# Two-layer decoder trunk: the second pair's values by quarters, two products sent to DRAM, four split tiles

## The chip, the cores and the metric

The kernel runs on one core of a Trainium2 chip. The metric is the device time of one execution in microseconds; of three runs of the kernel before, the median is 1551.42 us (1542.9 to 1553.19). Five engines work beside each other: TensorE (PE, matmuls), VectorE (DVE), ScalarE (ACT), GpSimd (POOL, here little more than an issuer of accumulating DMAs) and SyncE (SP, issuer of loads).

## The reference

Two layers over 512 tokens of width 1024. Each layer has a mixer (sliding-window attention and a retention, gated and merged) and an MLP; the change lies in the MLP and in the end of the program.

```python
def hybrid_layer(x, g_mix, w_in, sinks, w_a, w_b, w_out, g_mlp, w_up, w_down):
    h = rmsnorm(x, g_mix)
    z = h @ w_in
    ...
    mixed = jax.nn.sigmoid(ga) * ya + jax.nn.sigmoid(gb) * yb
    x = x + mixed @ w_out

    h2 = rmsnorm(x, g_mlp)
    x = x + jnp.square(jax.nn.relu(h2 @ w_up)) @ w_down
    return x

def reference(x, ...):
    for l in range(DEPTH):
        x = hybrid_layer(x, ...)
    return rmsnorm(x, g_final)
```

`w_up` is 1024 x 4096 and `w_down` 4096 x 1024. Everything is float32.

## The kernel before

**Split operands.** A float32 product is made of three matmuls: each operand is split into a high part (`hi`, `xh`, `r`) that the fast matmul format holds, and a low rest (`lo`, `xl`, `r`); `products` (L315) issues high x high, high x low and low x high, which are lines L321, L322 and L323. Weights come as units of 128 x 1024. For each, SP loads a tile `raw`; ACT writes `hi` (L275), DVE writes `lo` (L276). `unit` (L282) hands out one unit and splits up to two units beyond it; `split_until` (L259) loads up to four units beyond the one that it splits. There are six `raw` tiles and three of `hi` and of `lo`.

**The MLP.** x is held transposed in SBUF (8 tiles of 128 x 512). The 4096 hidden columns are eight blocks of 512 (`e` = 0 to 7). Because relu squared is homogeneous, the RMS factor is not put on the input: it is applied to the finished sum as a per-token `factor`, the inverse of mean square plus epsilon.

Products of 2 x 2 halves are computed by a scheme of seven products with sums of operands (Strassen-Winograd) in place of eight. For `e` > 0 two calls of `pair` (L1049) make the hidden values, 256 hidden columns each, from weight units with three and a half times 24 matmuls of 256 columns, in banks `a`, `e` and `b`, with `eu` as a holding place for two of them and `z` (128 x 2 x 512) for the result. `sums` holds the split sums of x's halves. `keep_up` (L1025) squares z. For the first pair it splits the left half of z (`first_hi`, `first_lo`) and the first sum; for the second pair it makes the other three sums (`Forms.rest`, L427), splits them, and splits z itself into `u_two`. For block 0, `group` makes four 128-column chunks in four PSUM banks together and `put_up` calls `keep_up` after chunks 1 and 3.

`down` (L1084) then multiplies with the block's part of `w_down` in seven steps of 12 matmuls of 512 columns: `b11` (first pair's left half), `u_forms[0]` (P5), `u_forms[1]` (giving U2), `b21`, `u_forms[2]`, `b22`, `u_forms[3]`. PSUM banks `a`, `b`, `c` come in twos, m = 0 and 1. P5 and U2 are copied from PSUM to SBUF by ACT. Four results per m (quadrants (0,0), (1,1), (0,1), (1,0) of tokens by columns) go through a `sink`: `Adding` (blocks 0 to 6) evacuates each to a tile `t`, by ACT where nothing is added, by DVE where P5 or U2 is added, and POOL sends it to a DRAM tile `y` with an adding DMA (L1148; block 0 writes plainly). `Ending` (block 7) loads `y` back, scales it by `factor` (`scale_all`; in the last layer `add_x` does it together with x), adds the last block's products on DVE (L1203, L1204). In layer 0 the result is transposed on PE and added to x (`turn`), and the next layer's first inputs are made (`ready`, `carry`); in the last layer x is transposed on PE and added to y (`add_x`, L1192 and L1196), then squared and summed (L1206), and the final norm and gain are applied (`output`, L1211) and stored.

**Buffers.** `temp` (tag `t`) has seven 128 x 512 tiles, which `eu`, P5, U2, the outgoing `y` tiles and short-lived others share in turn. `big` has six of 128 x 1024.

**Order.** The program is traced in the order of the source, and a scheduler then places the instructions on each engine by its own estimate of times. Each engine works through its list in order. A DMA that adds into DRAM is made to wait, on POOL, for earlier ones to the same rows.

Of the kernel before, what the change touches and what calls it, by code (L numbers as in the profile page):

```python
# [51 lines left out]
AHEAD = 5  # L52
# [51 lines left out]
def decoder(ctx, tc, xT, x_first, w_in, w_a, w_b, w_out, w_up, w_pair, w_down, tables, decay, band, g_last, out):  # L104
# [46 lines left out]
    def raw_tile():  # L151
        return wpool.tile([P, UNIT], F32, tag="raw", name="raw", bufs=6)
# [106 lines left out]
    def split_until(n):  # L259
        while state["split"] < min(n, len(order)):  # L260
# [8 lines left out]
            hi = wpool.tile([P, UNIT], F32R, tag="hi", name="hi")  # L269
            lo = wpool.tile([P, UNIT], F32R, tag="lo", name="lo")  # L270
# [128 lines left out]
    class Forms:  # L399
# [27 lines left out]
        def rest(self, ks, b, d, js):  # L427
            t1, t2, t3, t4 = (self.f[j // 2][:, 2 * (j % 2) : 2 * (j % 2) + 2, :] for j in range(4))
            b12, b21, b22 = b[:, :, H:], d[:, :, :H], d[:, :, H:]
            nc.vector.scalar_tensor_tensor(t2, t1, -1.0, b22, ALU.mult, ALU.subtract)  # L430
            self.keep(ks, 0, self.f[0], js)
            nc.vector.tensor_tensor(t3, b22, b12, ALU.subtract)
            nc.vector.scalar_tensor_tensor(t4, t2, -1.0, b21, ALU.mult, ALU.subtract)
            self.keep(ks, 2, self.f[1], (2, 3))
# [37 lines left out]
    class Rms:  # L472
# [8 lines left out]
        def finish(self):  # L481
            self.value = tmp.tile([P, T], F32, tag="rstd", name="rstd", bufs=2)
# [5 lines left out]
    def layer_body(layer):  # L488
# [501 lines left out]
        last = layer == DEPTH - 1  # L990
        sums = Forms((0, 2))
# [4 lines left out]
        columns = small.tile([P, 2 * NB], F32, tag="columns", name="columns", bufs=1)  # L996
        factor, negative = columns[:, :NB], columns[:, NB:]

        def column_factors():
# [4 lines left out]
            nc.vector.tensor_scalar(factor, ps[:, :NB], 1.0 / D, EPS, ALU.mult, ALU.add)  # L1004
            nc.vector.reciprocal(factor, factor)
            nc.vector.tensor_scalar(negative, factor, -1.0, None, ALU.mult)
            return ps

        def sum_input(ks):
# [7 lines left out]
            sums.rest(ks, *b, (0, 1))  # L1017
# [7 lines left out]
        def keep_up(z):  # L1025
            nc.scalar.activation(z, z, AF.Square)
            if not kept:
                split(first_hi, first_lo, z[:, :, :H])
                u_forms.one(0, z)
                u_forms.keep(0, 0, u_forms.f[0], (0,))  # L1030
                kept.append(z)
            else:
                u_forms.rest(0, kept.pop(), z, (1,))
                split(u_two[:, 0:2, :], u_two[:, 2:4, :], z)
# [3 lines left out]
        def put_up(c):  # L1038
            def put(ps):
# [4 lines left out]
                if c % 2:  # L1044
                    keep_up(z)
# [3 lines left out]
        def pair():  # L1049
# [20 lines left out]
            nc.scalar.activation(z[:, 0, :H], a, AF.Relu)  # L1070
            part = unit("pair", layer)
# [4 lines left out]
            nc.scalar.activation(z[:, :, H:], z[:, :, H:], AF.Relu)  # L1076
            part = unit("pair", layer)
            multiply(b, part, True, sums[3], False)
            nc.scalar.activation(z[:, 1, :H], b, AF.Relu, scale=-1.0)
            keep_up(z)  # L1080

        y = dram.tile([P, NB, D], F32, name=f"y{layer}")

        def down(e):  # L1084
# [22 lines left out]
            for m in range(2):  # L1107
                nc.scalar.activation(p5[m], c[m], AF.Copy)
# [21 lines left out]
        class Adding:  # L1130
# [7 lines left out]

            def put(self, i, j, m, ps, sign, more=None):
                t = temp("y")  # L1140
                if more is None:
                    nc.scalar.activation(t, ps, AF.Copy, scale=float(sign))  # L1142
                elif sign > 0:
                    nc.vector.tensor_tensor(t, ps, more, ALU.add)
                else:
                    nc.vector.scalar_tensor_tensor(t, ps, -1.0, more, ALU.mult, ALU.subtract)
                how = {"accum_op": ALU.add} if self.e else {}
# [4 lines left out]
        class Ending:  # L1152


            def __init__(self, e):
                sums.free()
                self.y, self.done = {}, {}
# [5 lines left out]
                if last:  # L1163
                    self.gain = big("gain")
                    nc.sync.dma_start(self.gain, g_last)
                    self.sq = small.tile([P, 4 * NB], F32, tag="sq", name="sq", bufs=1)
                else:
                    self.scale_all()

            def scale_all(self):  # L1170
# [4 lines left out]

            def begin(self, step):
                if last:
                    if step < 4:
                        self.add_x(*QUADS[step])
                elif step > 1:  # L1180
# [5 lines left out]

            def add_x(self, i, j):
                for m in range(2):
                    ps = bank(ps_mm if m else ps_aux, "xt")
                    block = 2 * j + m  # L1190
                    for k in range(4):
                        nc.tensor.transpose(  # L1192
                            ps[:, k * P : (k + 1) * P], x[:, 4 * i + k, block * P : (block + 1) * P], ident
                        )
                    v = self.y[i, j, m]
                    nc.vector.scalar_tensor_tensor(v, v, factor[:, block : block + 1], ps, ALU.mult, ALU.add)  # L1196

            def put(self, i, j, m, ps, sign, more=None):
# [6 lines left out]
                if last:  # L1205
                    nc.scalar.activation(temp("junk"), v, AF.Square, accum_out=self.sq[:, 2 * block + i : 2 * block + i + 1])  # L1206
                    self.done[i, j] = m
                    if (1 - i, j) in self.done and self.done[1 - i, j] >= m:
                        self.output(j, m)

            def output(self, j, m):  # L1211
                block = 2 * j + m
                total = self.sq[:, 2 * NB + block : 2 * NB + block + 1]
                nc.vector.tensor_tensor(total, self.sq[:, 2 * block : 2 * block + 1], self.sq[:, 2 * block + 1 : 2 * block + 2], ALU.add)
                nc.scalar.activation(total, total, AF.Sqrt, bias=eps, scale=1.0 / D)
                nc.vector.reciprocal(total, total)
                for i in range(2):
                    v = self.y[i, j, m]
                    nc.vector.scalar_tensor_tensor(v, v, total, self.gain[:, i, :], ALU.mult, ALU.mult)
                    (nc.sync if i else nc.scalar).dma_start(out[:, block, i * T : (i + 1) * T], v)  # L1220
# [15 lines left out]
            def ready(self, k):  # L1236
                scaled_input(k, g_mix + 2)
                squared_input(k, g_mix + 2)
                nc.sync.dma_start(spill[:, k, :], x[:, k, :])

            def carry(self):
                self.turn(1, 0)
                for k in range(4, KD):
                    self.ready(k)

        def first_hooks():
# [6 lines left out]
            def at1():  # L1253
                nc.tensor.matmul(used[0], ones, xh[:, 0, :], start=True, stop=True)
# [175 lines left out]
```

## Time and profile before

| | |
|---|---|
| runs, us | 1542.9, 1551.42, 1553.19 |
| profiled execution, us | 1553.22 |
| its span, us | 1551.4 |
| mean granted TensorE clock | 0.988 |
| MLP of layer 0 | about 422 to 757 us of the span |
| MLP of layer 1 | about 1186 us to the end |

The page gives one execution. A row of waits reads: engine, tile and line that waited, engine (or DMA), tile and line that ended the wait, total us, times, longest. A row of the timeline gives start, length, engine, line, operation, output and input tiles, count, and in brackets the idle time before it and what ended it. The row of a DMA queue has packets, MB and the share of 16 engines' time. PE's busy time includes pipelined matmuls' modelled ends, so the steps from start to start tell its pace.

### The profile page before, as it was taken

What the parts mean: (1) busy time and instruction counts of PE and PEld (TensorE: products, weight loads), DVE (VectorE), ACT (ScalarE), POOL (GpSimd) and SP (SyncE); (2) the same over time, 40 slices, a digit from 0 to 9 for tenths busy, and PEclk for the clock granted to TensorE, in tenths of its full rate; (3) what the DMA queues carried; (4) which work ended last, traced back from release to release, by engine and by line L of the source; (5) the groups of instructions that cost most, each with busy time, mean ns of one, the idle gap of its engine ahead of it and who ended that gap; (6) DMA issues with size and microseconds to landing.
All of it is one profiled execution on the core that took longest, in us unless ns stands there. A gap on an engine that the chain in (4) does not pass through costs nothing.

```text
span 1551.4 us, 21097 instructions
## 1 busy us (share of the span) xinstructions
PE 1488.0 (96%) x7766; PEld 1267.4 (82%) x7766; DVE 1108.5 (71%) x1622; ACT 900.0 (58%) x1429; POOL 172.5 (11%) x261
## 2 busy tenths in 40 slices
PE   9999999999999999999899999999999988999995
PEld 7888888888877888888788888888887877888884
DVE  6877567744867777767988765776557777777778
ACT  6657354622666676666765653554345756666664
POOL 0001111100011111111001012110000111001110
PEclk9999999999999999999999999999999999999998
DMA  7654998564235567776647489877532565566772
GB/s 255 196 154 139 264 253 214 154 195 129 96 116 145 160 172 183 184 184 171 236 124 199 126 224 261 206 185 202 157 115 75 175 143 134 156 166 184 183 194 99
DMA packets 92023, 267.88 MB, mean 173 GB/s; under 512 B 10640, under 2 KB 10768, under 8 KB 87824
## 3 DMA queue, kind: packets, MB, share of 16 engines
q1 hardware_dynamic: 63424, 172.94, 33.4%
q0 software_dynamic: 27776, 92.29, 28.2%
q8 instruction: 61, 1.00, 0.2%
q10 hardware_dynamic: 720, 1.31, 0.2%
q14 instruction: 42, 0.34, 0.1%
HBM read 230.32 MB, written 96.47 MB: 211 GB/s over the span
## 4 chain that ended last, share of the span: by engine, by line
PE 66%; issue 18%; DMA 4%; DVE 4%; ACT 4%; POOL 2%; DVEq 0%; ACTq 0%; SPq 0%; POOLq 0%
PE mm L323 18%; PE mm L321 18%; PE mm L322 18%; DMA y<-y 3%; POOL y L1148 2%; PE rv L321 2%; PE rv L322 2%; PE rv L323 2%; ACT hi L275 1%; DVE lo L276 1%; DMA dm<-decay_in 1%; PE score L660 1%; PE b L321 1%; PE pT L625 1%; PE b L322 1%
## 5 line engine op out<-in xcount | busy, mean ns | idle before, releaser
L275 ACT ACTIVATE hi<-raw 128x1024 fp32r<-128x1024 f32 (+1 forms) x366 | 373.2, 1020 | 400.6 <-PE mm L322 251.2
L276 DVE TENSOR_TENSOR lo<-raw,hi 128x1024 fp32r<-128x1024 f32 (+1 forms) x367 | 428.0, 1171 | 200.5 <-ACT hi L275 199.2
L323 PE MATMUL mm<-xh,lo 128*128 128x512 f32 (+1 forms) x1008 | 356.7, 357 | 8.9 <-DVE lo L276 8.9
L321 PE MATMUL mm<-xh,hi 128*128 128x512 f32 (+1 forms) x1008 | 356.8, 357 | 2.3 <-ACT xh L331 2.3
L322 PE MATMUL mm<-xl,hi 128*128 128x512 f32 (+1 forms) x1008 | 358.0, 357 | 0.5 <-DVE xl L332 0.5
L321 PE MATMUL mm<-r,hi 128*128 128x256 f32 (+1 forms) x768 | 252.7, 329 | 3.6 <-ACT mm L1063 3.6
L322 PE MATMUL mm<-r,hi 128*128 128x256 f32 (+1 forms) x768 | 252.0, 328 | 0.0
L323 PE MATMUL mm<-r,lo 128*128 128x256 f32 (+1 forms) x768 | 252.0, 328 | 0.0
L323 PEld LDWEIGHTS mm<-xh,lo 128*128 128x128 f32 x1008 | 191.5, 190 | 38.9 <-DVE lo L276 13.2
L321 PEld LDWEIGHTS mm<-xh,hi 128*128 128x128 f32 x1008 | 191.5, 190 | 28.7 <-ACT xh L331 3.4
L322 PEld LDWEIGHTS mm<-xl,hi 128*128 128x128 f32 x1008 | 191.8, 190 | 25.8 <-DVE xl L332 0.8
L1148 POOL DMA_DIRECT2D y<-y x112 | 93.6, 997 | 660.4 <-ACT y L1142 612.8
L321 PEld LDWEIGHTS mm<-r,hi 128*128 128x128 f32 x768 | 146.9, 191 | 17.8 <-ACT mm L1063 4.7
L322 PEld LDWEIGHTS mm<-r,hi 128*128 128x128 f32 x768 | 146.8, 191 | 12.8
L323 PEld LDWEIGHTS mm<-r,lo 128*128 128x128 f32 x768 | 146.8, 191 | 12.6
L321 PE MATMUL mm<-hi,r 128*128 128x512 f32 x256 | 96.8, 407 | 27.0 <-ACT r L328 27.0
L322 PE MATMUL mm<-lo,r 128*128 128x512 f32 x256 | 102.1, 399 | 0.0
L323 PE MATMUL mm<-hi,r 128*128 128x512 f32 x256 | 101.1, 407 | 0.8 <-DVE r L329 0.5
L321 PE MATMUL b<-hi,r 128*128 128x512 f32 x192 | 79.1, 412 | 4.7 <-ACT r L328 3.5
L321 PEld LDWEIGHTS mm<-hi,r 128*128 128x128 f32 x256 | 47.5, 194 | 41.1 <-ACT r L328 33.6
L322 PE MATMUL b<-lo,r 128*128 128x512 f32 x192 | 77.3, 402 | 0.0
L323 PE MATMUL b<-hi,r 128*128 128x512 f32 x192 | 72.3, 390 | 0.0
(204 smaller groups left out, 2161.9 us busy)
## 6 DMA issues: line engine op xcount, KB each, us to landing
raw<-w_in_in SPq DMA_DIRECT2D x89, 512.0 KB, 5.2
sums_down<-w_down_in POOLq DMA_DIRECT2D x32, 1024.0 KB, 10.8
sums_up<-w_pair_in POOLq DMA_DIRECT2D x56, 512.0 KB, 9.8
y<-y POOLq DMA_DIRECT2D x112, 256.0 KB, 7.3
raw<-w_down_in SPq DMA_DIRECT2D x48, 512.0 KB, 5.1
raw<-w_pair_in SPq DMA_DIRECT2D x84, 256.0 KB, 3.9
raw<-sums_down SPq DMA_DIRECT2D x32, 512.0 KB, 5.2
raw<-sums_up SPq DMA_DIRECT2D x56, 256.0 KB, 4.3
```

Of the source, the lines that this page charges most:

```text
L275: nc.scalar.activation(hi[:, at], raw[:, at], AF.Copy)
L276: nc.vector.tensor_tensor(lo[:, at], raw[:, at], f32(hi[:, at]), ALU.subtract)
L321: nc.tensor.matmul(ps, ah, bh, start=start and i == 0, stop=False, **more)
L322: nc.tensor.matmul(ps, ah, bl, start=False, stop=False, **more)
L323: nc.tensor.matmul(ps, al, bh, start=False, stop=stop and i == n - 1, **more)
L625: nc.tensor.transpose(pt[:, i * P : (i + 1) * P], sm[:, at : at + P], ident)
L660: nc.tensor.matmul(ps[:, g * w : (g + 1) * w], q_s[g][:, c, at], part[:, keys], start=i == 0, stop=i == 1)
L1148: nc.gpsimd.dma_start(y[:, 2 * j + m, i * T : (i + 1) * T], t, **how)
```

## The change

- `second`, `second_late` and `second_rest` replace the second half of `keep_up`: the second pair's value is squared and split in pieces as its quarters are finished, row 0's left half after the second part, the right halves after the third, row 1's left half at the end. `Forms.rest` becomes `middle` and `rest`.
- In `Adding`, P5 (with sign −1) and U2 are sent to DRAM as transfers of their own (`early`), so that all evacuations are plain ACT copies; each block has twelve transfers where it had eight.
- `hi` and `lo` have four tiles each and `raw` five; splitting runs three units ahead (`SPLIT`), loading three beyond that (`AHEAD`). `rstd` has one tile.
- Block 0 makes its chunks two by two (`two_chunks`), with `w_up` laid out to match.
- In the last layer, x is transposed during block 0, divided by `factor` and written to `y` (`turn_x`), and all later transfers add to it; `add_x` is gone. The end applies the gain on DVE before the norm is known and the norm on ACT after.
- `carry` makes all four inputs of the next layer before it squares them.

```diff
-AHEAD = 5
+AHEAD = 4
+SPLIT = 3
...
-        return wpool.tile([P, UNIT], F32, tag="raw", name="raw", bufs=6)
+        return wpool.tile([P, UNIT], F32, tag="raw", name="raw", bufs=5)
...
-            hi = wpool.tile([P, UNIT], F32R, tag="hi", name="hi")
-            lo = wpool.tile([P, UNIT], F32R, tag="lo", name="lo")
+            hi = wpool.tile([P, UNIT], F32R, tag="hi", name="hi", bufs=SPLIT + 1)
+            lo = wpool.tile([P, UNIT], F32R, tag="lo", name="lo", bufs=SPLIT + 1)
...
-        split_until(i + 3)
+        split_until(i + SPLIT + 1)
...
-    def two_chunks(name, layer, moving, evacuates):
+    def two_chunks(name, layer, moving, evacuates, meanwhile=None):
...
+            if meanwhile and u == 0:
+                meanwhile()
...
+        def middle(self, ks, b, d, js):
+            b12, b22 = b[:, :, H:], d[:, :, H:]
+            nc.vector.scalar_tensor_tensor(self.part(1), self.part(0), -1.0, b22, ALU.mult, ALU.subtract)
             self.keep(ks, 0, self.f[0], js)
+            nc.vector.tensor_tensor(self.part(2), b22, b12, ALU.subtract)
+
+        def rest(self, ks, d, js):
+            nc.vector.scalar_tensor_tensor(self.part(3), self.part(1), -1.0, d[:, :, :H], ALU.mult, ALU.subtract)
+            self.keep(ks, 2, self.f[1], js)
...
-            self.value = tmp.tile([P, T], F32, tag="rstd", name="rstd", bufs=2)
+            self.value = tmp.tile([P, T], F32, tag="rstd", name="rstd", bufs=1)
...
+        def turn_x(ps, b, i):
+            for k in range(4):
+                nc.tensor.transpose(ps[:, k * P : (k + 1) * P], x[:, 4 * i + k, b * P : (b + 1) * P], ident)
+            t = temp("y")
+            nc.scalar.activation(t, ps, AF.Copy, scale=inverse[:, b : b + 1])
+            nc.gpsimd.dma_start(y[:, b, i * T : (i + 1) * T], t)
...
-        def keep_up(z):
+        def first_two(z):
             nc.scalar.activation(z, z, AF.Square)
...
+        def second(z, rows, at):
+            nc.scalar.activation(z[:, rows, at], z[:, rows, at], AF.Square)
+            split(u_two[:, rows, at], u_two[:, slice(rows.start + 2, rows.stop + 2), at], z[:, rows, at])
+
+        TWO, LATE, SOON = slice(0, 2), slice(H, T), slice(0, H)
+
+        def second_late(z):
+            second(z, TWO, LATE)
+            u_forms.middle(0, kept[0], z, (1,))
+            u_forms.keep(0, 2, u_forms.f[1], (2,))
+
+        def second_rest(z):
+            kept.pop()
+            u_forms.rest(0, z, (3,))
...
             nc.scalar.activation(z[:, 0, :H], a, AF.Relu)
+            if which:
+                second(z, slice(0, 1), SOON)
...
             nc.scalar.activation(z[:, :, H:], z[:, :, H:], AF.Relu)
+            if which:
+                second_late(z)
...
             nc.scalar.activation(z[:, 1, :H], b, AF.Relu, scale=-1.0)
-            keep_up(z)
+            if which:
+                second(z, slice(1, 2), SOON)
+                second_rest(z)
+            else:
+                first_two(z)
...
             for m in range(2):
-                nc.scalar.activation(p5[m], c[m], AF.Copy)
+                sink.early(1, 1, m, p5[m], c[m], -1)
             multiply(b, u_forms[1], False)
             for m in range(2):
-                nc.scalar.activation(u2[m], b[m], AF.Copy)
+                sink.early(0, 1, m, u2[m], b[m], 1)
...
+            def early(self, i, j, m, t, ps, sign):
+                nc.scalar.activation(t, ps, AF.Copy, scale=float(sign))
+                self.send(i, j, m, t, last or self.e > 0)
+
             def put(self, i, j, m, ps, sign, more=None):
                 t = temp("y")
-                if more is None:
-                    nc.scalar.activation(t, ps, AF.Copy, scale=float(sign))
-                elif sign > 0:
-                    nc.vector.tensor_tensor(t, ps, more, ALU.add)
-                else:
-                    nc.vector.scalar_tensor_tensor(t, ps, -1.0, more, ALU.mult, ALU.subtract)
-                how = {"accum_op": ALU.add} if self.e else {}
+                nc.scalar.activation(t, ps, AF.Copy, scale=float(sign))
+                self.send(i, j, m, t, last or self.e > 0 or more is not None)
+
+            def send(self, i, j, m, t, add):
+                how = {"accum_op": ALU.add} if add else {}
                 nc.gpsimd.dma_start(y[:, 2 * j + m, i * T : (i + 1) * T], t, **how)
...
-                    nc.scalar.activation(temp("junk"), v, AF.Square, accum_out=self.sq[:, 2 * block + i : 2 * block + i + 1])
...
+                    nc.scalar.activation(temp("junk"), v, AF.Square, accum_out=both if ready else first)
+                    nc.vector.tensor_tensor(v, v, self.gain[:, i, :], ALU.mult)
+                    if not ready:
+                        nc.vector.tensor_scalar(first, first, 1.0 / D, EPS, ALU.mult, ALU.add)
+                        return
+                    nc.scalar.activation(total, both, AF.Sqrt, bias=first, scale=1.0 / D)
+                    nc.vector.reciprocal(total, total)
+                    for n in (1 - i, i):
+                        v = self.y[n, j, m]
+                        nc.scalar.activation(v, v, AF.Copy, scale=total)
+                        (nc.sync if n else nc.scalar).dma_start(out[:, block, n * T : (n + 1) * T], v)
...
                 for k in range(4, KD):
-                    self.ready(k)
+                    scaled_input(k, g_mix + 2)
+                for k in range(4, KD):
+                    self.rest(k)
...
-                group("w_up", layer, xs, [put_up(c) for c in range(4)], first_hooks())
+                hooks = first_hooks()
+                for c in (0, 2):
+                    two_chunks("w_up", layer, xs, [put_up(c), put_up(c + 1)], hooks[c // 2])
             else:
-                pair()
-                pair()
+                pair(0)
+                pair(1)
```

More of the change, by code (lines that the diff above doesn't have):

```diff
@@ L1174, in scale_all, with early @@
                         nc.scalar.activation(v, v, AF.Copy, scale=factor[:, 2 * j + m : 2 * j + m + 1])
+            def early(self, i, j, m, t, ps, sign):
+                nc.scalar.activation(t, ps, AF.Copy)
             def begin(self, step):
[L1177 to L1180, printed above, removed]
+                if not last and step > 1:
                     self.turn(*QUADS[step - 2])
@@ L1205, in put @@
                 if last:
[L1206 to L1220 removed]
+                    first, total, both = (self.sq[:, n * NB + block : n * NB + block + 1] for n in range(3))
+                    ready = (1 - i, j, m) in self.done
+                    self.done.add((i, j, m))
+                    nc.scalar.activation(temp("junk"), v, AF.Square, accum_out=both if ready else first)
[9 more added lines that the diff above has]
+                        (nc.sync if n else nc.scalar).dma_start(out[:, block, n * T : (n + 1) * T], v)
             def turn(self, i, j):
@@ L1253, in at1 @@
             def at1():
-                nc.tensor.matmul(used[0], ones, xh[:, 0, :], start=True, stop=True)
+                if last:
+                    used.append(bank(ps_aux, "xt"))
+                    for n in range(KD):
+                        turn_x(used[n % 2], n // 2, n % 2)
+                for ps in used:
+                    nc.tensor.matmul(ps, ones, xh[:, 0, :], start=True, stop=True)
                 sum_input(2)
```

66 lines of the change are left out of this document (26 added, 40 removed).

## The prediction

> **What bounds the kernel now.** I read the page's head first, then what TensorE (PE) waited for, and then the same waits by stage.
>
> ```profile
> span 1551.4 us, 21097 instructions
> PE 1488.0 (96%) x7766; PEld 1267.4 (82%) x7766; DVE 1108.5 (71%) x1622; ACT 900.0 (58%) x1429; POOL 172.5 (11%) x261
> ...
> PE mm L321 <- ACT r L328: 27.0, 16, 1.9
> PE mm L323 <- DVE lo L276: 8.9, 8, 2.3
> PE mm L321 <- ACT mm L1063: 3.6, 4, 1.7
> PE b L321 <- ACT r L328: 3.5, 13, 0.3
> ...
> PE mm L321 <- ACT r L328: 14.2, 8, 1.9
> ...
> PE mm L321 <- ACT r L328: 12.4, 7, 1.9
> ```
>
> PE is busy 96% of the span, so the time is the matmuls plus PE's stops. The first group of waits is the whole kernel; the last two lines are its largest entry again, for 422 to 757 us and 1186 to 1516 us, the two MLP stages. 26.6 of its 27.0 us lie there: the stops are in the eight MLP blocks of each layer (16 waits, 16 blocks), and the mixers have next to none. So the change can win only in the MLPs.
>
> One such stop, first on PE, then on ScalarE (ACT), below two narrow matmuls of a pair; columns are start and length in us, and in brackets the idle time before:
>
> ```profile
> 549.43 0.28 PE L321 MATMUL mm<-r,hi 128*128 128x256 f32 x1
> 549.55 0.28 PE L322 MATMUL mm<-r,hi 128*128 128x256 f32 x1
> ...
> 571.07 0.39 PE L322 MATMUL mm<-lo,r 128*128 128x512 f32 x1
> 571.30 0.39 PE L323 MATMUL mm<-hi,r 128*128 128x512 f32 x1
> 573.44 0.50 PE L321 MATMUL mm<-hi,r 128*128 128x512 f32 x1 [1.76 <-ACT r L328]
> 573.78 0.39 PE L322 MATMUL mm<-lo,r 128*128 128x512 f32 x1
> ...
> 574.24 0.40 PE L322 MATMUL mm<-lo,r 128*128 128x512 f32 x1
> 574.91 0.50 PE L321 MATMUL b<-hi,r 128*128 128x512 f32 x1 [0.27 <-ACT r L328]
> 575.25 0.40 PE L322 MATMUL b<-lo,r 128*128 128x512 f32 x1
> ...
> 570.02 0.36 ACT L1079 ACTIVATE z<-mm 128x256 f32<-128x256 f32 x1
> 570.41 1.06 ACT L1026 ACTIVATE z<-z 128x1024 f32<-128x1024 f32 x1
> 571.38 1.07 ACT L1108 ACTIVATE eu<-mm 128x512 f32<-128x512 f32 x2
> 572.33 1.06 ACT L328 ACTIVATE r<-z 128x1024 fp32r<-128x1024 f32 x1
> ```
>
> After the second pair's last product ACT does a relu, squares the whole 128x1024 value, copies P5 out, and splits the whole value. The split ends at 573.39, and PE, out of other work since 571.30, starts at 573.44. That is the wait of every block.
>
> **What the change takes away.** 512-wide matmuls start 571.30 − 571.07 = 0.23 us apart, 256-wide ones 0.12. The stop costs more than its idle time: 571.30 to 573.44 is 2.14 us for a wait of 1.76, and the next step is 0.34; the second stop takes 0.67 and then 0.34. Over a plain 0.23 that is 0.15 + 0.11 + 0.17 + 0.11 = 0.54 us of refilling a block, some 8 us in 15 blocks.
>
> After such stops PE also runs at half rate for a while, here in the block before, where starts come 0.43 apart:
>
> ```profile
> 531.41 0.80 PE L321 MATMUL b<-hi,r 128*128 128x512 f32 x1 [0.27 <-ACT r L328]
> 532.00 0.63 PE L322 MATMUL b<-lo,r 128*128 128x512 f32 x1
> 532.43 0.63 PE L321 MATMUL b<-hi,r 128*128 128x512 f32 x1
> 532.86 0.63 PE L322 MATMUL b<-lo,r 128*128 128x512 f32 x1
> ...
> 422.00:757.00 335.00, 314.39 (x1893) 275.05 (x1892) 247.75 (x293) 224.58 (x338) 47.72 (x57) 0.98 0.62 168
> 1186.00:1516.00 330.00, 307.64 (x1854) 270.96 (x1853) 234.76 (x278) 213.40 (x321) 46.81 (x56) 0.97 0.60 160
> 539.00:582.50 43.50, 41.47 (x260) 36.71 (x259) 33.13 (x40) 30.47 (x46) 8.21 (x10) 1.00 0.65 174
> ```
>
> In the last three lines (window, length, busy of PE, PEld, DVE, ACT, POOL, granted clock, DMA share, GB/s) the two MLPs have clocks of 0.98 and 0.97. Time lost is 0.02 x 335 + 0.03 x 330 = 16.6 us, by rounding 13 to 20; I take 14, and three quarters of it, 11 us, for the stops of the split (30.5 us of the 43 us of waits listed above). The Trainium skill, "TensorE: Matmul & The Clock Gate", section "Why this matters for your kernels", asks for no idle gaps over about 3 us, so by its rule a 1.76 us wait would cost no clock. Here the clock does fall behind stops of 1.76 and 0.27 us, so the trace does not bear it out; a rival below takes the other side.
>
> In the changed program the first-pair products, b11 and u_forms[0], stand on PE before the second pair's last product. Behind that product nothing is needed at once but row 0 of the second pair's value, which `second` squares and splits a quarter of a block earlier. Only the 128x256 corner of row 1 is left: relu 0.36, square and split of the same width about 0.37 each, by the 128x256 row at 570.02. PE meets it after 6 + 4 + 2 + 8 matmuls, 20 x 0.23 = 4.6 us. Even with ACT's queued work before it (an unpack of weights 1.06, two copies of 0.54) it is there after some 3.5 us. So the wait goes; if ACT ran 1.2 us later than so, it would begin to come back. In the first block of each layer four relus and squares stand together as now, with 24 x 0.23 = 5.5 us of b11 and u_forms[0] as cover; I leave 1 us there. Gain: 27.0 + 3.5 − 2 = 28.5 us.
>
> Next is the start of a pair, 8.9 + 3.6 = 12.5 us in the list. It comes from buffers that a DMA holds:
>
> ```profile
> 580.41 1.08 ACT L1142 ACTIVATE y<-mm 128x512 f32<-128x512 f32 x2
> ...
> 589.66 1.09 ACT L1142 ACTIVATE y<-b 128x512 f32<-128x512 f32 x2 [3.24 <-DMA y<-y]
> ...
> 581.35 2.65 POOL L1148 DMA_DIRECT2D y<-y  x3 [31.91 <-ACT y L1142]
> ...
> ACT y L1142 <- DMA y<-y: 32.8, 11, 3.8
> ...
> y<-y POOLq DMA_DIRECT2D x112, 256.0 KB, 7.3
> ```
>
> ACT stands 3.2 us until the second y(0,0) tile, issued about 581.9, has landed (7.7 us), and the weight splits queue behind it. A fourth split tile puts one more unit of weights, 24 x 0.12 = 2.9 us of pair matmuls, between that stop and PE, and DVE no longer waits for these buffers. Those 12.5 us go.
>
> **What it adds.** ACT takes over four 128x512 evacuations a block from DVE (0.54 us each in the pairs above) and about five small pieces, some 3 us on 30.5 busy in a block of 43.5, DVE loses as much: neither becomes the bound. P5 and U2 go out as accumulating DMAs, twelve a block for eight. All seven temp buffers are now freed by landings; twelve y tiles and two `eu` make exactly two rounds. So the last y(1,0) takes the buffer of the first y(0,0), and the next pair's `eu` that of the second. Between those copies PE has 24 x 0.12 + 12 x 0.23 = 5.6 us; the landing takes 7.7 and the issue about 1, so ACT still stands about 3 us, as now. What hangs on it is the copy that frees bank b: 3 us, then two `eu` copies (0.37, as the relu of 0.36 above) and an unpack (1.06, as the split of that width), 4.8 us, against 36 matmuls of 0.12 = 4.3 us of cover. That is 0.5 us a block; with twelve transfers queued I take 1.0, 14 us in 14 blocks. From below: nothing, if landings take 5 us. From above: 3 us a block, 42 us, if the whole stop showed. The Trainium skill, "DMA: Bandwidth & Descriptors", section "Anatomy of one DMA — SWDGE (gpsimd) path", has a fit of 2 us plus the bytes over 436 GB/s, 2.6 us for 256 KB; by that the ring would cost nothing and my sum be 14 us lower, but the landings here take 7.3.
>
> A put to quadrant (1,1) waits on POOL until P5 has landed in the same rows, with all later y transfers queued behind it; P5 leaves some 11 us earlier, more than 7.7, so nothing. Four more transfers on the DMA rings: the share is 0.65 of 43.5 us, 28 us a block; eight y are some 12 us of it (28.4% in the queue line below), four more 6 us, so 34 of about 40: hidden.
>
> ```profile
> q0 software_dynamic: 1152, 2.10, 28.4%
> ...
> 1535.75 0.60 PE L1192 MATMUL xt<-ident,x 128*128 128x128 f32 x4
> 1536.11 0.48 PE L321 MATMUL b<-hi,r 128*128 128x512 f32 x1
> ...
> 1537.35 0.40 PE L323 MATMUL b<-hi,r 128*128 128x512 f32 x1
> ...
> 1546.45 1.42 DVE L1219 SCALAR_TENSOR_TENSOR y<-y,sq,gain 128x512 f32<-128x512 f32 x2
> ...
> L1220 SPq DMA_DIRECT2D y_out<-y x4: 332/334/350, 1543.5 to 1547.9; - x4
> ```
>
> The transposes of x, eight groups of four at 0.36 (1536.11 − 1535.75), 2.9 us, move from the last block to the last layer's first: no change in sum, and their ACT copies and plain DMAs lie beside PE there. At the end, PE stops at 1537.7, and 13.7 us follow. In the changed program seven gain multiplications (0.71, by the pair of 1.42) and the reciprocals stand on DVE after the last put, then eight ACT multiplications (0.54), then four issues on ACT's queue (0.33): 0.9 + 5.0 + 0.3 + 4.3 + 1.3, and 1551.4 − 1547.9 = 3.5 us from the last issue to the end as now, 15.3: +1.5 us. The order of `carry` at the layer boundary may save 1 us; `w_up` by twos has the same matmuls, and the smaller `raw` and `rstd` rings free as early, since splitting runs a unit ahead.
>
> **Sum.** −28.5 − 8 − 11 − 12.5 + 14 + 1.5 − 1 = −45.5 us. The profiled execution took 1553.2 us, 1.8 above its span, which gives 1508; it lies 1.8 above the median of the runs, 1551.4, and against that it is 1506. Of three runs the fastest took 1542.9, as if with fewer slow stretches of the clock than the profiled one had; for that I give back 3 us and say 1509.
>
> **Rivals.** (1) The clock's half-rate stretches do not hang on these stops, the page's side: then 11 us stay, 1520. For it: the block of 539 to 582.5 us has the same 1.76 us stop and a clock of 1.00. (2) The buffer ring shows in full: +28 us over the forecast, 1537. For it: ACT's 3.2 us stops in 11 of 14 blocks; against: the weights are a unit further ahead. (3) Slower: the accumulate queue. Twelve transfers of some 2 us each in a burst make y(0,0) land late, the first `eu` of the next pair stands, and bank b with it. Each us of landing beyond the 8.2 that my 1.0 us stands for costs 14 us; the 42 us of the forecast are gone at 11.2 us. At the longest landing of a y transfer now,
>
> ```profile
> DMA to landing us min/median/max: 4.6/7.6/12.6
> ```
>
> 12.6 us (505 to 760 us, the last of a burst of eight), it gives 14 x 4.4 = 62 us more, 1571. Against: P5 and U2 go while the rings are quiet, and y(0,0) stands ahead of its burst. (4) The forecast without ring costs, 1495. That the new order stops PE just as before, so that nothing moves, is within (2).
>
> **How the numbers follow.** Forecast 0.58; (1) 0.12; (2) 0.14; (3) 0.08; (4) 0.08. The range 1492 to 1538 leaves out (3) and some of the ends of (2) and (4). What a measurement tells from no change is about 1%, 15.5 us: below 1536 is faster. Forecast, (1), (4) and a third of (2) give 0.83; the rest of (2) 0.09 no change; (3) 0.08.
>
> **What would show it.** Right: PE's wait for the split (`r` from ACT) under 5 us in all, clocks of 0.99 in both MLP stages, blocks of about 40.5 us. The ring: ACT's `eu` and y copies waiting on DMA y, and PE's waits naming `eu` copies or `lo`. Wrong would be blocks of 43 us or more with the split's wait gone.

## The result and the profile after

| | before | changed |
|---|---|---|
| median of 4 runs, us | 1549.32 (1542.9 to 1553.19) | 1506.76 (1505.61 to 1507.86) |
| profiled execution's span, us | 1551.4 | 1505.9 |
| mean granted TensorE clock | 0.988 | 0.994 |

The ratio is 0.9729, 95% interval 0.9693 to 0.9765: 42.6 us faster. The prediction said 1509.

The head of the changed kernel's page:

```profile
span 1505.9 us, 21268 instructions
...
PE 1472.5 (98%) x7767; PEld 1262.5 (84%) x7767; DVE 1067.4 (71%) x1604; ACT 945.4 (63%) x1586; POOL 228.8 (15%) x325
```

Span less PE's busy time is PE's idle time: 1551.4 − 1488.0 = 63.4 us before, 1505.9 − 1472.5 = 33.4 us now. So of 45.5 us, 30.0 are stops that went and 15.5 are busy time, at the same number of matmuls: the half-rate stretches and the refilling behind the stops.

What PE waited for in the changed kernel, and below it two entries of ACT and DVE that are used later (engine, tile and line that waited, what ended it: total us, times, longest):

```profile
PE mm L322 <- ACT eu L1096: 4.5, 7, 1.3
PE mm L322 <- ACT xh L332: 3.2, 2, 2.5
PE b L324 <- DVE r L330: 3.1, 6, 1.7
PE turn L1252 <- DVE x L1258: 2.4, 1, 2.4
...
PE mm L324 <- DVE lo L277: 0.7, 1, 0.7
...
ACT eu L1096 <- DMA y<-y: 15.7, 12, 2.7
...
DVE raw L237 <- DMA raw<-sums_up: 40.2, 15, 4.5
```

(Lines L321 to L323 of before are L322 to L324 here, and the split's L328 is L329.) The 27.0 and 3.5 us for `r` from ACT are gone from the list, as are the 3.6 us for `mm` from ACT, and `lo` falls from 8.9 to 0.7. New is `eu`, 4.5 us, and the low half of a split (`r` from DVE), 3.1 us, of which 1.7 stand at the boundary of the layers.

The two MLP stages of the changed kernel (window, length, busy us of PE, PEld, DVE, ACT and POOL, granted clock, DMA share, GB/s):

```profile
422.00:739.00 317.00, 313.34 (x1923) 278.83 (x1921) 239.68 (x300) 249.15 (x415) 72.14 (x85) 1.00 0.83 204
1160.00:1490.00 330.00, 323.89 (x1977) 286.84 (x1976) 239.56 (x302) 252.79 (x424) 78.54 (x92) 1.00 0.80 195
```

Beside the same view of before (clocks 0.98 and 0.97): PE's idle time in these stages was 335 − 314.39 = 20.6 and 330 − 307.64 = 22.4 us and is 3.7 and 6.1 us, and the clock is 1.00 in both. The DMA share went from 0.62 and 0.60 to 0.83 and 0.80, and ACT and POOL do more; none of that became the bound.

For the stages I took the starts of matching matmuls in PE's timeline: the MLP's first matmul (the column sums), the first and the last 128x256 high x high matmul with `xh` (the pairs of blocks 1 to 7), the next layer's first matmul with `xh`, and the last matmul. The columns from "four tiles" on are experiments told below.

| stage, us | before | changed | four tiles alone | whole value | quarters alone | three tiles | six buffers |
|---|---|---|---|---|---|---|---|
| both mixers | 839.9 | 841.8 | 841.7 | 838.0 | 838.4 | 840.8 | 841.2 |
| first blocks | 71.3 | 68.3 | 69.6 | 68.6 | 70.9 | 75.3 | 68.3 |
| blocks 1 to 7 | 566.1 | 523.1 | 604.3 | 602.5 | 535.8 | 536.8 | 538.8 |
| last `down` and boundary | 31.2 | 33.4 | 39.6 | 37.9 | 32.2 | 32.2 | 33.4 |
| last `down`, layer 1 | 28.8 | 23.6 | 30.8 | 29.3 | 25.8 | 26.3 | 23.6 |
| from the last matmul on | 14.1 | 15.6 | 14.9 | 13.3 | 16.4 | 14.4 | 15.4 |

Of the 45.5 us, 43.0 came out of blocks 1 to 7, 3.0 out of the first blocks, 5.2 out of the last `down`; 1.5 went into the end, 2.2 into the boundary of the layers and 1.9 into the mixers. The mixers of the kernels in this table lie between 838.0 and 841.8 us, so the last figure may be scatter.

### The profile page after: what moved, and what is told of

Same layout as the page of the kernel before. It is cut to its first block, busy times and chain, and to the rows that moved or that the text cites. A ratio compares the mean times of both kernels' runs of the same rounds, so it can differ in the third digit from the quotient of the medians.

```text
span 1505.9 us, 21268 instructions
## 1 busy us (share of the span) xinstructions
PE 1472.5 (98%) x7767; PEld 1262.5 (84%) x7767; DVE 1067.4 (71%) x1604; ACT 945.4 (63%) x1586; POOL 228.8 (15%) x325
## 4 chain that ended last, share of the span: by engine, by line
PE 80%; DMA 7%; DVE 6%; ACT 4%; issue 2%; POOL 0%; ACTq 0%; DVEq 0%
PE mm L322 21%; PE mm L323 21%; PE mm L324 21%; DMA raw<-w_down_in 3%; DVE lo L277 2%; PE b L324 2%; DMA y<-y 2%; PE b L322 2%; PE b L323 2%; PE rv L322 2%; PE rv L323 2%; PE rv L324 2%; DMA dm<-decay_in 1%; ACT hi L276 1%; PE score L667 1%
## 5 line engine op out<-in xcount | busy, mean ns | idle before, releaser
L322 PE MATMUL mm<-xh,hi 128*128 128x512 f32 (+1 forms) x1008 | 358.4, 359 | 7.7 <-ACT eu L1096 4.5
L323 PE MATMUL mm<-xl,hi 128*128 128x512 f32 (+1 forms) x1008 | 358.1, 357 | 0.0
L324 PE MATMUL mm<-xh,lo 128*128 128x512 f32 (+1 forms) x1008 | 356.2, 357 | 0.0
L324 PE MATMUL mm<-r,lo 128*128 128x256 f32 (+1 forms) x768 | 251.3, 327 | 0.7 <-DVE lo L277 0.7
L323 PE MATMUL mm<-r,hi 128*128 128x256 f32 (+1 forms) x768 | 251.1, 327 | 0.0
L322 PE MATMUL mm<-r,hi 128*128 128x256 f32 (+1 forms) x768 | 251.0, 327 | 0.0
L322 PEld LDWEIGHTS mm<-xh,hi 128*128 128x128 f32 x1008 | 191.6, 190 | 35.6 <-ACT eu L1096 6.2
L323 PEld LDWEIGHTS mm<-xl,hi 128*128 128x128 f32 x1008 | 191.8, 190 | 25.7
L324 PEld LDWEIGHTS mm<-xh,lo 128*128 128x128 f32 x1008 | 191.2, 190 | 25.2
L323 PEld LDWEIGHTS mm<-r,hi 128*128 128x128 f32 x768 | 145.7, 190 | 14.8
L322 PEld LDWEIGHTS mm<-r,hi 128*128 128x128 f32 x768 | 145.7, 190 | 14.6
L324 PEld LDWEIGHTS mm<-r,lo 128*128 128x128 f32 x768 | 145.7, 190 | 13.4 <-DVE lo L277 0.9
L1187 POOL DMA_DIRECT2D y<-y x112 | 98.3, 1206 | 66.2 <-ACT y L1182 65.9
L1187 POOL DMA_DIRECT2D y<-eu x56 | 47.3, 852 | 396.5 <-ACT eu L1177 372.7
L324 PE MATMUL mm<-hi,r 128*128 128x512 f32 x256 | 95.3, 391 | 0.5 <-DVE r L330 0.5
L323 PE MATMUL mm<-lo,r 128*128 128x512 f32 x256 | 95.7, 390 | 0.0
L322 PE MATMUL mm<-hi,r 128*128 128x512 f32 x256 | 91.5, 394 | 0.1
L322 PE MATMUL b<-hi,r 128*128 128x512 f32 x192 | 76.3, 398 | 0.2 <-ACT y L1182 0.2
L324 PE MATMUL b<-hi,r 128*128 128x512 f32 x192 | 73.2, 396 | 3.1 <-DVE r L330 3.1
L323 PE MATMUL b<-lo,r 128*128 128x512 f32 x192 | 75.2, 392 | 0.0
```

The source lines that it names most:

```text
L322: nc.tensor.matmul(ps, ah, bh, start=start and i == 0, stop=False, **more)
L323: nc.tensor.matmul(ps, ah, bl, start=False, stop=False, **more)
L324: nc.tensor.matmul(ps, al, bh, start=False, stop=stop and i == n - 1, **more)
L1187: nc.gpsimd.dma_start(y[:, 2 * j + m, i * T : (i + 1) * T], t, **how)
```

## Experiments

Each kernel was compared with runs of the kernel before on the same chip; ratios are to that. Every one of them computes the whole reference. None of the ones called "the changed kernel with ..." has any other edit.

### The second pair's value whole again, and the early transfers back

The changed kernel with the second pair's value squared and split in one piece at its end:

```diff
+        def second_whole(z):
+            nc.scalar.activation(z, z, AF.Square)
+            u_forms.middle(0, kept.pop(), z, (1,))
...
+            split(u_two[:, 0:2, :], u_two[:, 2:4, :], z)
...
-                second(z, slice(1, 2), SOON)
-                second_rest(z)
+                second_whole(z)
```

> The changed kernel, but the second pair's value is squared and split whole at its end, as before. If the gain is that of the quarters (theory): TensorE waits for the split again in each of 16 blocks, 20 to 30 us in all, with stretches of half clock back in both MLP stages (granted 0.97 to 0.98), and the time is 1535 to 1550. If the gain came from the early transfers and the fourth split tile (rival): 1507 to 1515, with a clock of 0.99.

Measured: 1591.35 us, ratio 1.0275 (1.0223 to 1.0328), slower than the kernel before and above both ranges. The first entry of PE's waits, and one of ACT's:

```profile
PE mm L322 <- ACT r L329: 51.1, 14, 3.6
...
ACT y L1182 <- DMA y<-y: 8.4, 13, 1.3
```

and its MLP stages in the view of stretches:

```profile
422.00:757.00 335.00, 307.38 (x1832) 272.92 (x1831) 216.90 (x252) 230.45 (x352) 70.81 (x84) 0.96 0.69 177
1180.00:1515.00 335.00, 305.57 (x1761) 268.59 (x1761) 217.75 (x256) 225.28 (x343) 69.28 (x82) 0.96 0.66 170
```

The quarters are worth 85 us in this kernel, not the 47.5 (28.5 + 8 + 11) of my terms: 14 waits of up to 3.6 us where before had 16 of up to 1.9. And the clock is at 0.96 with these waits, where it was 1.00 without: the half-rate stretches hang on these stops.

The changed kernel with P5 and U2 kept in SBUF and added by DVE, as before:

```diff
-                nc.scalar.activation(t, ps, AF.Copy, scale=float(sign))
-                self.send(i, j, m, t, last or self.e > 0)
+                nc.scalar.activation(t, ps, AF.Copy)
...
+                elif sign > 0:
+                    nc.vector.tensor_tensor(t, ps, more, ALU.add)
+                else:
+                    nc.vector.scalar_tensor_tensor(t, ps, -1.0, more, ALU.mult, ALU.subtract)
```

> The changed kernel, but P5 and U2 stay in SBUF and DVE adds them, eight transfers a block as before. If the quarters carry the gain (theory): 1505 to 1517, a few us of pair-start waits back or none. If moving the additions off DVE carries it (rival): 1525 or more, with TensorE waiting for lo from DVE.

Measured: 1511.47 us (1510.54 to 1516.46), 0.9768 (0.9724 to 0.9812). The medians are 4.7 us apart; the runs of the two do not overlap, the intervals of the ratios do. Its waits on PE, of the line that the changed kernel has not:

```profile
PE b L322 <- DVE y L1186: 6.6, 12, 1.1
```

PE now waits for bank b until DVE has combined it with P5 (L1186). Sending the pieces early takes that wait away. Its worth is not told apart from nothing by the ratios: 4.7 us by the medians, 2.8 by the profiled executions.

### The fourth split tile

The changed kernel with three tiles of `hi` and `lo`, six of `raw`, as before; then the same with one temp buffer more:

```diff
-AHEAD = 4
-SPLIT = 3
+AHEAD = 5
+SPLIT = 2
...
-        return wpool.tile([P, UNIT], F32, tag="raw", name="raw", bufs=5)
+        return wpool.tile([P, UNIT], F32, tag="raw", name="raw", bufs=6)
```

```diff
-        return tmp.tile([P, T], F32, tag="t", name=name, bufs=7)
+        return tmp.tile([P, T], F32, tag="t", name=name, bufs=8)
```

> The changed kernel with three split tiles, six raw tiles and splitting two units ahead. If the fourth tile is what removed the 12.5 us of waits at the start of a pair (theory): 1512 to 1525, TensorE waiting 5 to 15 us for lo or for copies from ACT. If it adds nothing to the other parts (rival): 1505 to 1510.

> Three split tiles as in the run before it, and eight temp buffers in place of seven. If ACT's stops behind buffers that transfers hold are what remains at the start of a pair (theory): ACT's waits on DMA y fall by half or more, and the time is 4 to 12 us under the run with three split tiles and seven buffers. If they are hidden anyway (rival): the same within 2 us.

Measured: 1529.6 us, 0.9884 (0.9839 to 0.9930), with three tiles; 1525.26 us, 0.9854 (0.9807 to 0.9901), with eight buffers also. The first is above both of its ranges. The runs of the two overlap, so what the eighth buffer is worth in time is not shown; its effect on the waits is. Waits with three tiles (PE, ACT, DVE):

```profile
PE mm L324 <- DVE lo L277: 16.5, 13, 1.7
PE mm L322 <- ACT mm L1094: 6.1, 10, 1.1
...
ACT y L1182 <- DMA y<-y: 23.6, 11, 2.7
...
DVE raw L237 <- DMA raw<-sums_up: 43.0, 14, 4.1
```

and with the eighth buffer, where ACT's wait for DMA y and PE's for L1094 are gone:

```profile
PE mm L324 <- DVE lo L277: 19.0, 14, 2.1
...
DVE raw L237 <- DMA raw<-sums_up: 44.0, 14, 3.8
```

So the two waits at the start of a pair, which the prediction put down to one cause, have two in these kernels. The copies of `mm` stand behind buffers that landings hold. The `lo` waits do not: they stay without that hold. DVE stands at the addition of two weight units (L237) until a load of `sums_up` is in, 14 times, and `lo` is queued behind. The changed kernel has the same stop of DVE (40.2 us, 15 times); the fourth tile does not shorten it, it covers it.

The kernel before with the fourth tile and its rings alone (the diff above the other way round, on the old program, with `rstd` at one tile):

> The kernel before with four split tiles and five raw tiles alone. Theory: the waits at the start of a pair (12.5 us) go, the split's waits stay or grow, because the first pair's products are then placed ahead of the second pair's last one and no longer cover it: 1540 to 1590. Rival: what made the whole-value run slow is the early transfers, so that this one is at 1530 to 1542.

Measured: 1601.33 us, 1.0321 (1.0290 to 1.0352): 51 us slower, and above both ranges. Its waits on PE, with one of ACT's, and its MLP stages:

```profile
PE mm L322 <- ACT r L329: 52.7, 16, 3.6
PE mm L322 <- ACT mm L1064: 15.5, 11, 2.3
...
ACT y L1143 <- DMA y<-y: 65.4, 23, 5.9
```

```profile
422.00:757.00 335.00, 302.92 (x1789) 271.00 (x1788) 227.23 (x269) 207.45 (x312) 46.65 (x56) 0.95 0.58 152
1180.00:1520.00 340.00, 311.24 (x1775) 274.14 (x1773) 237.56 (x284) 212.03 (x316) 39.74 (x48) 0.95 0.52 144
```

One of these stops, in the timeline of PE and then of ACT:

```profile
577.44 0.28 PE L324 MATMUL mm<-r,lo 128*128 128x256 f32 x1
581.37 0.80 PE L322 MATMUL mm<-hi,r 128*128 128x512 f32 x1 [3.65 <-ACT r L329]
581.97 0.63 PE L323 MATMUL mm<-lo,r 128*128 128x512 f32 x1
582.39 0.63 PE L322 MATMUL mm<-hi,r 128*128 128x512 f32 x1
```

```profile
577.82 1.04 ACT L276 ACTIVATE hi<-raw 128x1024 fp32r<-128x1024 f32 x1
578.77 0.37 ACT L1080 ACTIVATE z<-mm 128x256 f32<-128x256 f32 x1
579.17 1.06 ACT L1027 ACTIVATE z<-z 128x1024 f32<-128x1024 f32 x1
580.26 1.06 ACT L329 ACTIVATE r<-z 128x1024 fp32r<-128x1024 f32 x1
```

In the prediction's stop (kernel before, 571 us) 512-wide products of the first pair's value stand directly ahead of it, and there the stop is 1.76 us. Here the last matmul ahead of the stop is a narrow one: with a unit more in hand, the built program has put those wide products ahead of the second pair's last product. Nothing is left behind it to cover an unpack, a relu, a square and a split of ACT, 0.95 + 0.40 + 1.09 + 1.06 = 3.5 us. The whole-value kernel above has the same 3.6 us, with ACT's waits for DMA y at 8.4 us where this one's are 65.4: so the 3.6 us come from the order and the whole value, not from ACT standing.

### Quarters alone

The kernel before with the second pair's value in quarters, and nothing else:

```diff
-            else:
-                u_forms.rest(0, kept.pop(), z, (1,))
-                split(u_two[:, 0:2, :], u_two[:, 2:4, :], z)
...
+        def second(z, rows, at):
+            nc.scalar.activation(z[:, rows, at], z[:, rows, at], AF.Square)
+            split(u_two[:, rows, at], u_two[:, slice(rows.start + 2, rows.stop + 2), at], z[:, rows, at])
```

> The kernel before with one part of the change alone: the second pair's value squared, split and summed by quarters. If the quarters by themselves remove the stop at the split (theory): its waits fall from 30 us to under 5, the waits at the start of a pair stay at 10 to 25 us, and the time is 1512 to 1530. If the quarters need the fourth tile or the early transfers to work (rival): 1535 or more, the split's waits still over 15 us.

Measured: 1523.55 us, 0.9823 (0.9796 to 0.9851): 27 us faster. Its waits on PE and ACT:

```profile
PE mm L321 <- ACT mm L1083: 20.3, 12, 2.0
...
PE mm L321 <- ACT r L328: 3.8, 2, 1.9
...
ACT y L1170 <- DMA y<-y: 31.9, 13, 2.9
```

The stops of the split fall from 27.0 to 3.8 us, and 20.3 us for copies of `mm` come up where before had 3.6: with its stop gone, PE meets the start of the next pair sooner than ACT, which stands for landings there (31.9 us, 13 times), has copied. So the parts do not add: quarters alone −27, the fourth tile alone +51, and all parts together −43.

### The ring of temp buffers

The changed kernel with six temp buffers:

```diff
-        return tmp.tile([P, T], F32, tag="t", name=name, bufs=7)
+        return tmp.tile([P, T], F32, tag="t", name=name, bufs=6)
```

> The changed kernel with six temp buffers for seven. If landings of the y transfers hold ACT, and through it TensorE, as the prediction priced it (theory): ACT's waits on DMA y at least double and TensorE's waits for copies into eu rise from 4.5 us to 15 or more, 1515 to 1530. If the fourth split tile hides them (rival): 1505 to 1510.

Measured: 1520.98 us, 0.9818 (0.9789 to 0.9846), 14 to 16 us over the changed kernel. Its waits on PE and ACT:

```profile
PE mm L322 <- ACT eu L1096: 14.9, 13, 2.1
...
ACT eu L1096 <- DMA y<-y: 21.6, 13, 3.1
...
ACT y L1182 <- DMA y<-y: 12.6, 20, 1.4
```

With seven, ACT stands 15.7 us before `eu` and 1.2 us before `y` for the same landings, and PE waits 4.5 us for `eu`, of which not all is the ring. Two of those waits in the changed kernel's ACT timeline:

```profile
503.26 0.38 ACT L1096 ACTIVATE eu<-mm 128x256 f32<-128x256 f32 x1 [2.65 <-DMA y<-y]
...
1383.00 1.06 ACT L276 ACTIVATE hi<-raw 128x1024 fp32r<-128x1024 f32 x1 [0.36 <-DMA raw<-w_down_in]
1383.97 0.37 ACT L1096 ACTIVATE eu<-mm 128x256 f32<-128x256 f32 x1
```

The first is the ring: ACT stands 2.65 us for a landing, and 0.86 of it reaches PE. In the second ACT had nothing to do with a landing of y: it stood for a load of weights, and the unpack (1.06 us) ran ahead of the copy. By such rows four of the seven waits (0.86, 0.16, 0.23 and 0.50 us) belong to the ring, 1.8 us. So the mechanism is there, and at seven buffers it costs 2 to 5 us; one buffer fewer brings it out in full.

### The small parts

The order of `carry` as before; the end's last multiplications shared between ACT and DVE; block 0's four chunks together; the changed kernel once more, and the first two of these edits together:

```diff
                 for k in range(4, KD):
-                    scaled_input(k, g_mix + 2)
-                for k in range(4, KD):
-                    self.rest(k)
+                    self.ready(k)
```

```diff
-                        nc.scalar.activation(v, v, AF.Copy, scale=total)
+                        if n == i:
+                            nc.vector.tensor_scalar(v, v, total, None, ALU.mult)
+                        else:
+                            nc.scalar.activation(v, v, AF.Copy, scale=total)
```

```diff
-                for c in (0, 2):
-                    two_chunks("w_up", layer, xs, [put_up(c), put_up(c + 1)], hooks[c // 2])
+                group("w_up", layer, xs, [put_up(c) for c in range(4)], hooks)
```

> The changed kernel with the old order of carry: each input of the next layer is squared and stored directly after it is made. TensorE loses some 9 us between the layers in the changed kernel (waits of 1.7, 2.4 and 2.5 us and a half-rate stretch). If the new order of carry makes that (rival): 1500 to 1504. If it does not, since the waits before it stand on turn and on the last sums (theory): 1505 to 1510.

> The changed kernel, but at the end DVE does one of the two last multiplications by the norm of each block of tokens and ACT the other. If ACT's eight multiplications set the tail (theory): 2 to 3 us less than the changed kernel, 1503 to 1505. If the stores do (rival): 1506 to 1508.

> The changed kernel with block 0's four chunks made together, as before. If making them by twos took the stop of 1.9 us out of each layer's first block (theory): 3 to 7 us slower than the changed kernel, 1510 to 1514, with a wait of some 2 us in each first block. If the quarters alone do that (rival): within 1.5 us.

> The changed kernel again, beside the three runs that follow, for a comparison on one chip: 1505 to 1509.

> The changed kernel with the old order of carry and the last multiplications shared by DVE and ACT, the two edits that were 1 to 3 us faster alone. If these are gains (theory): 2 to 5 us under the changed kernel run beside it. If they were scatter between chips and runs, as the stage lengths suggest, where the boundary and the tail each moved by 0.5 us or less (rival): within 1.5 us of it.

| kernel | median, us | ratio (95%) |
|---|---|---|
| changed, again | 1505.33 | 0.9723 (0.9697 to 0.9748) |
| old order of `carry` | 1505.26 | 0.9711 (0.9679 to 0.9742) |
| end shared by ACT and DVE | 1503.51 | 0.9695 (0.9668 to 0.9722) |
| four chunks together | 1505.32 | 0.9721 (0.9694 to 0.9748) |
| `carry` and end together | 1504.04 | 0.9706 (0.9683 to 0.9729) |

None of them is told apart from the changed kernel. By the stages: the boundary is 33.4 us with either order of `carry`. With four chunks together layer 0's first block is 34.7 us for 31.9 (a stop of 1.9 us for `r` is back), and the span about as long. The shared end took the part behind the last matmul from 15.6 to 15.1 us, where four fewer ACT multiplications might have given 2. The stores, in the view of that tile for the changed kernel, then for the shared end (SP's four; the landings are those of all eight):

```profile
L1244 SPq DMA_DIRECT2D y_out<-y x4: 332/334/350, 1497.4 to 1501.7; - x4
...
DMA to landing us min/median/max: 2.0/2.4/2.6
```

```profile
L1247 SPq DMA_DIRECT2D y_out<-y x4: 332/362/1138, 1494.4 to 1496.0; - x4
...
DMA to landing us min/median/max: 2.1/3.7/4.9
```

SP's four are issued within 1.6 us in place of 4.3, and the eight stores land a median of 3.7 us after their issue, for 2.4. With all of them issued by 1496.2 us and the span at 1502.5, the end then waits for the stores, no longer for ACT.

## Why the prediction was right, point by point

**The split's wait.** Right: of 30.5 us none is left in the list. Less the 3.1 us of new waits for `r` from DVE that is 27.4 us, for my 28.5. How much the chain could cost was mis-read: I took the stop of before, 1.76 us, for its price, and the experiments with the fourth tile show 3.6 us once no wide product covers it.

**The clock.** Right, and the first rival falls: in the blocks the half-rate stretches went with the stops, and came back with them in the whole-value and four-tile kernels (0.96 and 0.95). The mean clock over the whole span gives 0.012 x 1551 = 18.6 us lost before and 0.006 x 1506 = 9.0 now. But part of that lies behind the last matmul, where a slow clock costs nothing: the granted clock is 0.64 in the last 13.7 us before and 0.61 in the last 15.2 us now, 4.9 and 5.9 us. Counted by stretches, the clock records of before have eight in the MLPs, each 3.41 us long at 0.50, 13.7 us lost; now there is one, 6.83 us at the boundary of the layers, 3.4 us. That is some 10 us gained, for my 11.

The Trainium skill, "TensorE: Matmul & The Clock Gate", section "What's actually happening", tells of a gate that throttles after an idle window of some 3.4 us, on a window that runs freely. The trace agrees on the window: each of the eight stretches is 3.41 us long, and they start whole multiples of 3.41 us apart (531.30, 661.01 and 749.76 us lie 38 and 26 of them apart). It does not agree that the window has to be idle throughout: in the 3.41 us ahead of each of the eight, PE stood idle for 1.7 to 2.3 us, about half. So a stop of 1.76 us, just at that edge, may cost clock or not. The one at 571 us, in the block whose clock of 1.00 the first rival had for it, fell to two windows, 0.58 and 1.18 us, and cost none. Of the stops that lay whole in one window some cost a stretch and some did not (702.78 us), and no run here shows the exact limit.

**Refilling.** Busy time fell by 15.5 us; less some 10 for the clock, 5 are left for the term of 8. The two cannot be told apart better.

**The start of a pair.** Right in size, wrong in part of the cause. The 12.5 us fell to 0.7, and the fourth tile did it. The 3.6 us for `mm` are as said: ahead of each of the four waits ACT stands 2.9 to 3.8 us for a landing. The 8.9 us for `lo` are mixed. One of these eight waits, in DVE's timeline of before:

```profile
585.53 0.69 DVE L236 TENSOR_TENSOR raw<-raw 128x512 f32<-128x512 f32 x1 [1.24 <-DMA raw<-sums_up]
586.99 0.69 DVE L1144 TENSOR_TENSOR y<-mm,eu 128x512 f32<-128x512 f32 x1 [0.76 <-DMA y<-y]
587.59 1.22 DVE L276 TENSOR_TENSOR lo<-raw,hi 128x1024 fp32r<-128x1024 f32 x1
```

Here DVE stands first for a load of weight sums and then for a buffer that a landing holds. Six of the eight waits, 4.7 us, are like it, with the landing last. In the other two, 2.3 and 1.9 us, DVE's last stop is at the addition of weight units: 4.2 us that are not the buffers. What I had not seen at all: the fourth tile without the quarters loses 51 us. My sum took its 12.5 us as a part of its own; its worth hung on another term.

**The ring.** The term that was mis-sized: 14 us priced, 2 to 5 measured. The landings as a whole were about as long as I took them:

```profile
DMA to landing us min/median/max: 2.6/7.0/16.1
```

That is y from 430 to 740 us, in the changed kernel. But the one that `eu` waits for, the second y(0,0), stands at the front of its burst, and in the seven blocks of layer 0 it landed a median of 6.4 us after its issue, where I took 7.7. So ACT does stand, but 15.7 us in 12 waits, 1.3 each, where I had 3 us in every block. That the unit more in `hi` and `lo` covers most of the rest is argued, not shown. Rivals (2) and (3) fall with it: the longest landing is past the 11.2 us at which (3) began to decide, but that price was for a late y(0,0), and in layer 0 its second tile landed after 7.8 us at most. Rival (4), no ring cost, is 1495: nearer in mechanism than the forecast, yet the time is not its.

**What ate the rest.** The waits that I summed (−28.5 − 12.5 + 14 + 1.5 − 1 = −26.5) measure −30.0 in PE's idle time, the busy terms (−19) measure −15.5: 3.5 us off each way. The end is as said: PE stops at 1490.7 and 15.2 us follow, for 15.3. The boundary has the wrong sign. It is 2.2 us longer. PE's timeline there, first before, then in the changed kernel:

```profile
768.75 1.21 PE L321 MATMUL mm<-xh,hi 128*128 128x512 f32 x4 [1.76 <-ACT xh L331]
```

```profile
736.67 0.50 PE L324 MATMUL b<-hi,r 128*128 128x512 f32 x1 [1.66 <-DVE r L330]
...
739.13 2.40 PE L1252 MATMUL turn<-ident,y 128*128 128x128 f32 x20 [0.34 <-DVE y L1229]
743.97 0.66 PE L1252 MATMUL turn<-ident,y 128*128 128x128 f32 x4 [2.44 <-DVE x L1258]
747.11 2.08 PE L322 MATMUL mm<-xh,hi 128*128 128x512 f32 x4 [2.49 <-ACT xh L332]
...
750.26 0.63 PE L324 MATMUL mm<-xh,lo 128*128 128x512 f32 x1
750.69 0.63 PE L323 MATMUL mm<-xl,hi 128*128 128x512 f32 x1
```

The stop for `xh`, 1.76 us before, is now 2.49, and comes behind one of 2.44 for x and one of 1.66 for a low half: twenty transposes stand together at 739.13, with no products among them, and the last four wait for x. Behind these stops the matmuls run 0.43 apart, at half rate. With the old order of `carry` the stage is as long, so that is not the cause. The kernel with quarters alone has twenty transposes together too (from 750.24 us), with stops of 1.28 us for x and 3.62 us for `xh` behind them, and the one with the fourth tile alone has them apart: the quarters' edit is enough to set them together.

Blocks are 40.1 and 40.6 us long in layer 1 (the same matmul of `down` at 1235.33, 1315.56 and 1396.79, two blocks apart), for 40.5. That the sum of −45.5 us is also what the two spans differ by is luck: the ring cost 9 to 12 us less than priced, and the new waits for `r`, the boundary, the refilling and the clock made that up.

## What to carry to other kernels

Price a chain by its own length and its cover separately: a wait seen in a trace is what is left after the cover, and a deeper look-ahead can take the cover away. So an edit that lets a scheduler run further ahead can lose alone what it wins together with another; before adding up parts, ask of each which wait the others uncover. And where a ring of buffers comes out exactly even, try it one smaller: that shows whether its edge is near and what it costs to cross it.

## What was not expected of the hardware

The changed kernel's MLPs, with stops of 1.3 us or less on PE and one of 1.66, ran at a clock of 1.00; a stop of 1.76 us cost clock in some blocks of before, and those of 3.6 us brought 0.95 to 0.96 over a whole MLP. In the kernel before, the half-rate stretches start on a grid of 3.41 us, behind windows in which PE was idle for about half. Transfers to y, most of them accumulating, that took a median of 7.0 us from issue to landing, and up to 16.1, left PE 3.7 us of idle time in an MLP with a DMA share of 0.83. The stores at the end landed a median of 1.3 us later when they were issued in under half the time.
